# Sums of weight quarters by accumulating DMAs instead of GpSimd, in a two-layer trunk on one core

## The chip, the cores and the metric

The kernel runs on one core of a Trainium2 chip. The core has a matrix engine (TensorE, PE in the profile), three engines for elementwise work (VectorE or DVE, ScalarE or ACT, GpSimd or POOL), and a queue engine (SyncE, SP) that issues most transfers. All transfers are carried by 16 DMA engines that the queues share. The metric is device time in microseconds; the kernel before takes 1237.47 us in the median of three runs (1236.72 to 1238.4).

## The reference

The input x has 512 tokens of 1024 features. There are two layers, each with a mixer, an MLP and a gate; every one of them sits between RMS norms and is added to x. All is float32.

```python
for i in range(2):
    m = fox_attention(hn, ...) if i == 0 else short_conv(hn, ...)     # hn = rmsnorm(x, g[0])
    x = x + rmsnorm(m, g[1])
    f = jnp.square(jax.nn.relu(rmsnorm(x, g[2]) @ w_mlp_up[i])) @ w_mlp_down[i]
    x = x + rmsnorm(f, g[3])
    gate = jax.nn.sigmoid(rmsnorm(x, g[4]) @ w_ple_gate[i])
    x = x + rmsnorm((p[i] @ w_ple_proj[i]) * gate, g[5])
```

The up weight is 1024 x 4096, the down weight 4096 x 1024. The change concerns the down weight, `wdn` in the kernel.

## The kernel before, in words

**Precision.** Each float32 matrix is split in two parts of a shorter type that the matrix engine multiplies faster: `split` (L272, L273) has ScalarE write the high part `wh` and another engine subtract it from the source to give the low part `wl`. `mm3` (L264 to L266) then issues three matmuls per product: high by high, low by high, high by low.

**The MLP.** The 4096 hidden features go in eight groups of 512 per layer, `up(gr)` and then `down(gr)`. In `up`, four tiles f = 0 to 3 of 128 features are computed over all 512 tokens with 24 matmuls each; ScalarE applies relu and square (L825, L811). For groups 0 to 6 `down` is a fast matrix product of the Strassen-Winograd kind: with the activations cut in quarters A11 to A22 and the group's down weight in quarters B11 to B22, seven products of half size replace eight. It needs four sums of activations, S1 to S4, which GpSimd forms in `quarters` (L839) as each f is done, and four sums of weights, T1 to T4. Each T is two tiles of 128 x 512 (p = 0, 1). The products run in the order of `STEPS`: 1 (B11), 2 (B21), 4 (T4), 5 (T1, with S1), 6 (T2), 7 (T3), 3 (B22), with 12 matmuls each. Their results are summed over the groups in `acc`, and after group 6 `combine` (L878) adds the seven sums up on GpSimd. Group 7 is an ordinary product.

**The weights' way.** Every weight tile is an item in one list in the order of use. `prepare` walks it a few items ahead of use (`SOON` = 8): `fetch` (L157) has SP load the 256 KB tile into one of 14 `raw` buffers, and `split` puts the halves into two of 70 `pages`, buffers of 2 KB per partition that almost everything shares. When `prepare` reaches a group's first down item, `derive` has all eight quarter tiles loaded and has GpSimd form the T tiles, eight subtractions of 128 x 512 per group (L167); GpSimd also splits the T tiles (L273, eight per group). Fourteen groups use it, seven per layer.

**What orders the work.** Only parts of the attention's start and end are written in a fixed order. Elsewhere a scheduler, which works from estimates of the instructions' times, orders each engine's instructions at build time; an instruction whose buffer is free early can be placed far ahead of its use. On the chip each engine and each queue runs its list strictly in that order. SP has at most eight transfers under way: each waits for the eighth before it.

**The start.** The attention's first stage norms four blocks of 128 tokens, t = 0 to 3. For each, ScalarE sums squares (L295), GpSimd forms the reciprocal root `n_r` in two small instructions (L287, L290), VectorE scales the block to `n_h` (L303), TensorE transposes it (`n_p`, L312), and ScalarE and VectorE split it into `hTh` and `hTl`. The orders of TensorE, VectorE and ScalarE are written out there; GpSimd's and SP's are not. VectorE's list has `n_h` of t = 3 ahead of `hTl` of t = 2. TensorE computes the values `v` of block t in between.

Of the kernel before, what the change touches and what calls it, by code (L numbers as in the profile page):

```python
# [8 lines left out]
F32 = mybir.dt.float32  # L9
F32R = mybir.dt.float32r  # L10
AF = mybir.ActivationFunctionType
ALU = mybir.AluOpType
# [3 lines left out]
P = 128  # L16
D = 1024
S = 512
# [7 lines left out]
PUT_OFF = 46000  # L26
LAG = 2
AHEAD = 2
PAGES = 70
RAWS = 14  # L30
LEAD = 1
V_CHUNKS = ((768, 272), (0, 512), (512, 256))
# [13 lines left out]
PRODUCTS = {  # L46
    1: ("A11", "B11"), 2: ("A12", "B21"), 3: ("S4", "B22"), 4: ("A22", "T4"),
    5: ("S1", "T1"), 6: ("S2", "T2"), 7: ("S3", "T3"),
}
STEPS = (1, 2, 4, 5, 6, 7, 3)  # L50
# [18 lines left out]
def trunk(ctx: ExitStack, tc, x, pT, g, wv, wqk, bf, wo, wci, wcq, cw, wco, wup, wdn, wpp, wpg, out):  # L69
    nc = tc.nc  # L70
    pool = lambda name, bufs, **k: ctx.enter_context(tc.tile_pool(name=name, bufs=bufs, **k))
    consts = pool("consts", 1)
    raws = pool("raws", RAWS)
    normed = pool("normed", 1)
    pages = pool("pages", PAGES)
    small = pool("small", 8)
    psum = pool("psum", 8, space=PSUM)
    dram = pool("dram", 1, space=DRAM)

    def page(name, dtype=F32):  # L80
        return pages.tile([P, S], dtype, tag="pg", name=name)
# [14 lines left out]
    loads, order, where, ready, fetched, begun = [], [], {}, {}, [], [0]  # L96
    derived, recipes = {}, {}
# [9 lines left out]
    def plan_sums(key, forms, quarters, sums):  # L107


        at = {}  # L110
        for name, src in quarters:
            at[name] = len(loads)
            loads.append(src)
        for name in forms:
            where[(*key, *name)] = len(order)
            order.append(((*key, *name), at.get(name, key)))
        recipes[key] = at, sums

    def plan_down(l, gr):

        plan_sums(
            ("dn", l, gr),
            [(PRODUCTS[i][1], p) for i in STEPS for p in range(2)],
            [
                ((name, p), wdn[l, c, 4 * gr + 2 * p + r])
                for name, r, c in (("B11", 0, 0), ("B21", 1, 0), ("B12", 0, 1), ("B22", 1, 1))
                for p in range(2)
            ],
            [
                ((name, p), (a, p), (b, p), ALU.subtract)  # L130
                for p in range(2)
                for name, a, b in (("T1", "B12", "B11"), ("T3", "B22", "B12"),
                                   ("T2", "B22", "T1"), ("T4", "B21", "T2"))
            ],
        )

    def plan_sevens(key, srcs):
        plan_sums(
# [18 lines left out]
            nc.sync.dma_start(raw[:, : src.shape[-1]], src)  # L157

    def derive(key):
        at, sums = recipes.pop(key)  # L160
        fetch(max(at.values()) + 1)
        B = {name: fetched[n][:, :S] for name, n in at.items()}
        for name, a, b, op in sums:
            t = page("_".join(str(u) for u in (*key, *name)))
            derived[(*key, *name)] = t
            B[name] = t[:, :S]
            ins = nc.gpsimd.tensor_tensor(out=B[name], in0=B[a], in1=B[b], op=op)  # L167
            if last_norm:
                tc.add_manual_dep(
                    ins.ins, last_norm.pop().ins.name,  # L170
                    mybir.DependencyInfo(mybir.DependencyClass.Sync, mybir.DependencyReason.DATA),
                )
# [30 lines left out]
    for l in range(2):  # L203
# [10 lines left out]
        else:  # L214
# [3 lines left out]
            for i in range(2, KT, 2):  # L218
                for name in "ucb":
                    s = "cub".index(name)  # L220
# [586 lines left out]
    def mlp(l, hT, xs, then, late):  # L807
        acc = {}
# [27 lines left out]
        def quarters(gr, f, q, s, A):  # L836

            L, R = slice(0, S // 2), slice(S // 2, S)
            sums = lambda out, a, b, op: nc.gpsimd.tensor_tensor(out=out, in0=a, in1=b, op=op)  # L839
            if f % 2 == 0:  # L840
                s[f] = page(f"s34{l}_{gr}_{f}")
                sums(s[f][:, L], q[f][:, L], q[f][:, R], ALU.subtract)
                return
            left, right = q[f - 1], q[f]
            halves(gr, f, ("A12", "A22"), right, A)
            s12, s34 = page(f"s12{l}_{gr}_{f}"), s[f - 1]
            sums(s12[:, L], left[:, R], right[:, R], ALU.add)
            sums(s12[:, R], s12[:, L], left[:, L], ALU.subtract)
            sums(s34[:, R], right[:, L], s12[:, R], ALU.subtract)
            halves(gr, f, ("S1", "S2"), s12, A)  # L850
            halves(gr, f, ("S3", "S4"), s34, A)
# [21 lines left out]
        def combine():  # L873

            for s in range(2):
                for to, i in ((2, 1), (6, 1), (7, 6), (4, 7), (6, 5), (3, 6), (5, 7)):
                    a = acc[to, s][:, :S]
                    nc.gpsimd.tensor_tensor(out=a, in0=a, in1=acc[i, s][:, :S], op=ALU.add)  # L878
            return {
                (2 * half + s, n): acc[i, s]  # L880
                for s in range(2) for i, half, n in ((2, 0, 0), (3, 0, 1), (4, 1, 0), (5, 1, 1))
            }

        for gr in range(7):
            A, s, q = {}, {}, {f: page(f"q{l}_{gr}_{f}") for f in range(4)}
# [9 lines left out]
            down(gr, A)  # L895

        total, hs, gB = combine(), [], []

        def done(f, lo, hi, r):
# [12 lines left out]
        for t in range(NB):  # L912
# [6 lines left out]
            for n in range(2):  # L919
                a = total[t, n][:, :S]  # L920
                nc.vector.tensor_tensor(out=a, in0=banks[n], in1=a, op=ALU.add)
            fs = [total[t, n][:, :S] for n in range(2)]
            sums = [squares(f, f"fs{l}_{t}_{n}") for n, f in enumerate(fs)]
# [183 lines left out]
```

## Time and profile before

| | |
|---|---|
| median of three runs | 1237.47 us (1236.72 to 1238.4) |
| profiled execution: its span (no other time is recorded for it) | 1235.8 us |
| TensorE matmul busy | 1213.4 us, 98% |
| VectorE, ScalarE, GpSimd busy | 896.5, 676.1 and 686.8 us |
| moved by DMA | 148.73 MB, 120 GB/s in the mean |
| granted TensorE clock | 0.998 |

The span is from the first to the last instruction; the runs' median lies 1.67 us above it. Busy time is a sum over instructions; the list of waits tells how long an engine stood before an instruction and what released it. In a timeline row the first number is the start in us, the second the duration of the row's instructions together, and xN their count; idle time ahead of them stands in brackets.

### The profile page before, as it was taken

To read this page: it belongs to the slowest core of one execution; us is meant where nothing else is said; L and a number is where in the kernel's file an instruction comes from. 1 tells how busy PE (TensorE), PEld (TensorE's weight loads), DVE (VectorE), ACT (ScalarE), POOL (GpSimd) and SP (SyncE) were. 2 spreads that over 40 slices of the span, in tenths; PEclk is the share of its full clock that TensorE was granted. 3 is DMA by queue.
4 is the path that set the end of the run, shared out by engine and by line. 5 is a ranking of instruction groups with operands and counts; after the bars stand their busy time and mean duration, and the time that the engine had idled before them with its cause. 6 is when DMAs were issued, how large, how long until landed. Compare 5 with 4: busy or idle time off the path is not lost.

```text
span 1235.8 us, 18684 instructions
## 1 busy us (share of the span) xinstructions
PE 1213.4 (98%) x6188; PEld 1030.6 (83%) x6188; DVE 896.5 (73%) x1394; ACT 676.1 (55%) x1429; POOL 686.8 (56%) x667
## 2 busy tenths in 40 slices
PE   7999999999999999999999999999999999999997
PEld 6888888888888888888889999989778888888885
DVE  5657878675667667869877798865767787669873
ACT  5457777556635654465566544445756345635551
POOL 2016667247878777775213255317778868778210
PEclk9999999999999999999999999999999999999999
DMA  7456564442343224428133033552412443235401
GB/s 253 150 160 169 147 159 114 151 164 66 115 137 98 88 88 136 123 69 288 67 102 107 27 107 96 154 176 71 136 59 78 137 136 95 66 114 178 163 18 52
DMA packets 85793, 148.73 MB, mean 120 GB/s; under 512 B 10112, under 2 KB 17328, under 8 KB 85696
## 3 DMA queue, kind: packets, MB, share of 16 engines
q1 hardware_dynamic: 85488, 147.27, 38.7%
q8 instruction: 49, 0.80, 0.3%
q14 instruction: 48, 0.39, 0.1%
q10 hardware_dynamic: 144, 0.26, 0.1%
q0 software_dynamic: 64, 0.00, 0.0%
HBM read 136.93 MB, written 6.37 MB: 116 GB/s over the span
## 4 chain that ended last, share of the span: by engine, by line
PE 89%; DVE 3%; POOL 2%; ACT 2%; issue 2%; DMA 2%; SPq 0%; POOLq 0%; DVEq 0%; ACTq 0%
PE up L266 9%; PE up L265 9%; PE up L264 9%; PE dn L265 8%; PE dn L266 8%; PE dn L264 8%; PE pg L265 2%; PE pg L264 2%; PE pg L266 2%; PE qk L264 2%; PE qk L265 2%; PE qk L266 2%; PE co L264 1%; PE co L266 1%; PE co L265 1%
## 5 line engine op out<-in xcount | busy, mean ns | idle before, releaser
L273 DVE TENSOR_TENSOR wl<-raw,wh 128x512 fp32r<-128x512 f32 (+1 forms) x398 | 370.2, 975 | 27.5 <-ACT wh L272 26.3
L272 ACT CAST wh<-raw 128x512 fp32r<-128x512 f32 (+1 forms) x398 | 217.1, 620 | 4.6 <-DVE xd L348 4.4
L265 PE MATMUL up<-hTh,wl 128*128 128x512 f32 (+1 forms) x576 | 210.2, 365 | 0.0
L266 PE MATMUL up<-hTl,wh 128*128 128x512 f32 (+1 forms) x576 | 209.7, 366 | 0.3 <-DVE hTl L273 0.3
L264 PE MATMUL up<-hTh,wh 128*128 128x512 f32 (+1 forms) x576 | 209.4, 366 | 0.0
L273 POOL TENSOR_TENSOR wl<-dn_T,wh 128x512 fp32r<-128x512 f32 x112 | 155.0, 1417 | 32.6 <-ACT wh L272 32.6
L825 ACT ACTIVATE r<-up 128x512 f32<-128x512 f32 (+1 forms) x72 | 39.4, 547 | 200.4 <-PE up L266 200.4
L871 DVE TENSOR_TENSOR acc<-dn,acc 128x512 f32<-128x512 f32 x168 | 107.2, 678 | 23.9 <-PE dn L266 23.9
L265 PEld LDWEIGHTS up<-hTh,wl 128*128 128x128 f32 x576 | 108.6, 189 | 17.7
L264 PEld LDWEIGHTS up<-hTh,wh 128*128 128x128 f32 x576 | 108.6, 189 | 17.5
L266 PEld LDWEIGHTS up<-hTl,wh 128*128 128x128 f32 x576 | 108.3, 189 | 17.9 <-DVE hTl L273 0.5
L167 POOL TENSOR_TENSOR dn_T<-raw,raw 128x512 f32<-128x512 f32 x56 | 87.5, 1575 | 58.9 <-DMA raw<-in_wdn 39.6
L167 POOL TENSOR_TENSOR dn_T<-raw,dn_T 128x512 f32<-128x512 f32 x56 | 93.3, 1666 | 2.2
L272 ACT CAST wh<-dn_T 128x512 fp32r<-128x512 f32 x112 | 61.4, 616 | 11.0 <-POOL dn_T L167 11.0
L273 DVE TENSOR_TENSOR A12l<-q,A12h 128x512 fp32r<-128x512 f32 x28 | 23.3, 833 | 51.7 <-ACT A12h L272 51.7
L273 DVE TENSOR_TENSOR A11l<-q,A11h 128x256 fp32r<-128x256 f32 x28 | 25.9, 926 | 45.5 <-ACT A11h L272 45.5
L878 POOL TENSOR_TENSOR acc<-acc,acc 128x512 f32<-128x512 f32 x28 | 46.9, 1706 | 9.9 <-DVE acc L871 9.9
L264 PE MATMUL qk<-hTh,wh 128*128 128x512 f32 x128 | 51.1, 399 | 0.0
L266 PE MATMUL qk<-hTl,wh 128*128 128x512 f32 x128 | 50.8, 397 | 0.0
L265 PE MATMUL pg<-wh,hTl 128*128 128x512 f32 x128 | 50.5, 394 | 0.0
L264 PE MATMUL pg<-wh,hTh 128*128 128x512 f32 x128 | 50.4, 394 | 0.0
L265 PE MATMUL qk<-hTh,wl 128*128 128x512 f32 x128 | 50.2, 393 | 0.0
(372 smaller groups left out, 3240.3 us busy)
## 6 DMA issues: line engine op xcount, KB each, us to landing
raw<-in_wup SPq DMA_DIRECT2D x128, 256.0 KB, 3.0
raw<-in_wdn SPq DMA_DIRECT2D x128, 256.0 KB, 2.9
raw<-in_wcq SPq DMA_DIRECT2D x36, 256.0 KB, 2.9
raw<-in_wqk SPq DMA_DIRECT2D x32, 256.0 KB, 3.6
raw<-in_wpg SPq DMA_DIRECT2D x32, 256.0 KB, 4.0
g<-in_g SPq DMA_DIRECT2D x22, 256.0 KB, 5.8
prl<-neg_c SPq DMA_DIRECT2D x16, 256.0 KB, 7.0
raw<-in_wo SPq DMA_DIRECT2D x16, 256.0 KB, 4.0
```

The lines of the kernel that those rows point to most:

```text
L167: ins = nc.gpsimd.tensor_tensor(out=B[name], in0=B[a], in1=B[b], op=op)
L264: nc.tensor.matmul(ps, a.hi, b.hi, start=start, stop=False)
L265: nc.tensor.matmul(ps, a.lo, b.hi, start=False, stop=False)
L266: nc.tensor.matmul(ps, a.hi, b.lo, start=False, stop=stop)
L272: nc.scalar.copy(hi, src)
L273: eng.tensor_tensor(out=lo, in0=src, in1=hi.bitcast(F32), op=ALU.subtract)
L825: nc.scalar.activation(r[:, :n], ps[:, :n], AF.Relu)
L871: nc.vector.tensor_tensor(out=a, in0=banks[s], in1=a, op=ALU.add)
L878: nc.gpsimd.tensor_tensor(out=a, in0=a, in1=acc[i, s][:, :S], op=ALU.add)
```

## The change

The sums T1 to T4 are no longer formed by GpSimd instructions. For each T, both tiles together, SP loads one quarter (512 KB, two rows of 2 KB per partition) into a buffer of a new pool `sums` of five buffers, and a DMA issued from GpSimd's queue adds the second term to it in place: from HBM for T1 and T3, from the buffer of T1 for T2 and of T2 for T4. [...] B12 is no longer loaded as tiles of its own, since only the T need it. GpSimd still splits the T tiles. The wait that held the first sum behind the last norm is gone from this part. `PAGES` falls from 70 to 60, which pays for the five buffers.

```diff
-PAGES = 70
+PAGES = 60
+SUMS = 5
...
+    def add_up(l, gr):
+
+        block = lambda r, c: wdn[l, c, 4 * gr + r : 4 * gr + r + 3 : 2].rearrange("k p c -> p k c")
+        B11, B21, B12, B22 = (block(r, c) for c in range(2) for r in range(2))
+        T = {}
+        for name, first, second in (("T1", B11, B12), ("T3", B12, B22),
+                                    ("T2", B22, "T1"), ("T4", B21, "T2")):
+            T[name] = t = sums.tile([P, 2, S], F32, tag="sum", name=f"{name}_{l}_{gr}")
+            nc.sync.dma_start(t, first)
+            second = T[second] if isinstance(second, str) else second
+            nc.gpsimd.dma_start(t, second, accum_op=ALU.add)
+        for name, t in T.items():
+            for p in range(2):
+                derived["dn", l, gr, name, p] = t[:, p, :]
...
     def derive(key):
+        if key[0] == "dn":
+            add_up(*recipes.pop(key))
+            return
         at, sums = recipes.pop(key)
...
-                sums(s[f][:, L], q[f][:, L], q[f][:, R], ALU.subtract)
+                sums(s[f][:, L], q[f][:, R], q[f][:, L], ALU.subtract)
...
-            sums(s12[:, L], left[:, R], right[:, R], ALU.add)
-            sums(s12[:, R], s12[:, L], left[:, L], ALU.subtract)
+            sums(s12[:, L], right[:, R], left[:, R], ALU.subtract)
+            sums(s12[:, R], s12[:, L], left[:, L], ALU.add)
...
-                for to, i in ((2, 1), (6, 1), (7, 6), (4, 7), (6, 5), (3, 6), (5, 7)):
-                    a = acc[to, s][:, :S]
-                    nc.gpsimd.tensor_tensor(out=a, in0=a, in1=acc[i, s][:, :S], op=ALU.add)
+                for to, i, j, op in (
+                    (2, 2, 1, ALU.add), (6, 6, 1, ALU.subtract), (7, 7, 6, ALU.add),
+                    (4, 4, 7, ALU.subtract), (6, 6, 5, ALU.subtract), (3, 3, 6, ALU.add),
+                    (5, 7, 5, ALU.subtract),
+                ):
+                    a, b, c = (acc[k, s][:, :S] for k in (to, i, j))
+                    nc.gpsimd.tensor_tensor(out=a, in0=b, in1=c, op=op)
```

More of the change, by code (lines that the diff above doesn't have):

```diff
@@ L119, in plan_down @@
     def plan_down(l, gr):
[L121 to L135, printed above, removed]
+        key = "dn", l, gr
+        at = {}
+        for name, r, c in (("B11", 0, 0), ("B21", 1, 0), ("B22", 1, 1)):
+            for p in range(2):
+                at[name, p] = len(loads)
+                loads.append(wdn[l, c, 4 * gr + 2 * p + r])
+        for i in STEPS:
+            for p in range(2):
+                name = PRODUCTS[i][1]
+                where[(*key, name, p)] = len(order)
+                order.append(((*key, name, p), at.get((name, p), key)))
+        recipes[key] = l, gr
+    def add_up(l, gr):
[9 more added lines that the diff above has]
+        for name, t in T.items():
+            for p in range(2):
+                derived["dn", l, gr, name, p] = t[:, p, :]
     def plan_sevens(key, srcs):
```

1 line of the change is left out of this document (added).

## The prediction

> **What bounds the kernel now.** I read the page's busy times first, then the list of TensorE's waits, then busy time by stage.
>
> ```profile
> PE 1213.4 (98%) x6188; PEld 1030.6 (83%) x6188; DVE 896.5 (73%) x1394; ACT 676.1 (55%) x1429; POOL 686.8 (56%) x667
> ```
> ```profile
> PE dn L264 <- ACT r L825: 1.1, 2, 0.9
> ...
> PE dn L265 <- DVE S1l L273: 0.8, 2, 0.4
> ...
> PE dn L265 <- DVE A12l L273: 0.4, 1, 0.4
> PE up L266 <- DVE hTl L273: 0.3, 1, 0.3
> ```
> ```profile
> core 0: us, PE busy (x) PEld busy (x) DVE busy (x) ACT busy (x) POOL busy (x), PEclk, DMA share, GB/s
> 275.00:300.00 25.00, 24.01 (x157) 21.36 (x157) 14.23 (x14) 14.84 (x34) 21.82 (x20) 1.00 0.22 65
> 300.00:382.00 82.00, 81.51 (x358) 66.58 (x357) 51.34 (x61) 50.39 (x95) 65.64 (x50) 1.00 0.33 103
> 382.00:590.00 208.00, 208.00 (x920) 172.22 (x919) 160.73 (x198) 107.27 (x198) 151.09 (x115) 1.00 0.43 136
> 850.00:870.00 20.00, 19.62 (x122) 17.10 (x121) 9.24 (x10) 10.57 (x24) 17.19 (x16) 1.00 0.23 66
> 870.00:952.00 82.00, 81.24 (x356) 66.34 (x356) 57.78 (x60) 51.72 (x98) 64.72 (x51) 1.00 0.34 103
> ```
>
> TensorE is the bound: 1213.4 of 1235.8 us. In the MLP's later groups (382 to 590) it has no idle time at all, and a matmul takes 208/920 = 0.226 us. What idles in the two MLPs is 0.99 + 0.49 us in the first groups of layer 0 and 0.38 + 0.76 us in those of layer 1, 2.62 us together. Whatever the change frees on GpSimd can give back 2.62 us at most; the rest of its work lies beside a full TensorE. A delay at the kernel's start, ahead of all this, is added to the end whole.
>
> **GpSimd's relief: 0 to -2.62 us, taken as -1.0.**
>
> ```profile
> L167 POOL TENSOR_TENSOR dn_T<-raw,raw 128x512 f32<-128x512 f32 x56 | 87.5, 1575 | 58.9 <-DMA raw<-in_wdn 39.6
> L167 POOL TENSOR_TENSOR dn_T<-raw,dn_T 128x512 f32<-128x512 f32 x56 | 93.3, 1666 | 2.2
> ```
>
> 112 subtractions go, 87.5 + 93.3 = 180.8 us of GpSimd, 12.9 us per group. The splits of the T stay. In a first group the eight sums stand at the head of a chain (sums, casts, splits, activation sums) that ends in the waits on r, S1l and A12l above. In the changed program the sums of layer 0's first group are placed in the attention's first 40 us and those of layer 1's at the end of layer 0's MLP, so this head is gone. The waits named add up to 2.3 us, but they are on ScalarE's and VectorE's work, whose queues also change order here. I take 1.0 of the 2.62, about the wait on r.
>
> **The start: this is the term that decides.** The five `sums` buffers are free from the beginning, so the scheduler has placed five of the new loads and five accumulating DMAs at the kernel's start. Two places in the built order matter. SP has the load of T1 at the place where the small load `taps` stood (taps moves behind). GpSimd has the accumulation of T1 between the `n_r` of block 2 and that of block 3, and GpSimd must stand there until the T1 load has landed. Behind it wait `n_r` of block 3, then `n_h` of block 3, and behind that, in VectorE's written order, `hTl` of block 2, which TensorE needs next.
>
> ```profile
> 16.71 0.33 SPq L685 DMA_DIRECT2D taps<-in_cw  x1
> 17.44 1.01 SPq L157 DMA_DIRECT2D raw<-in_wv  x2
> 18.78 25.31 SPq L157 DMA_DIRECT2D raw<-in_wqk  x18
> ```
> ```profile
> raw<-in_wdn SPq DMA_DIRECT2D x128, 256.0 KB, 2.9
> ...
> taps<-in_cw SPq DMA_DIRECT2D x1, 12.0 KB, 5.0
> ```
> ```profile
> 15.00:20.00 5.00, 3.99 (x25) 3.21 (x25) 3.78 (x6) 3.77 (x10) 1.73 (x4) 1.00 1.05 391
> ```
> ```profile
> 20.33 0.30 POOL L287 TENSOR_SCALAR n_r_v<-n_q,n_q 128x1 f32<-128x1 f32 x1 [2.74 <-ACT junk L295]
> 20.71 0.56 POOL L290 TENSOR_TENSOR n_r_y<-n_r_v,neg_half 128x1 f32<-128x1 f32 x1
> 21.23 0.53 POOL L643 MEMSET ones<- 128x512 f32 x1
> ```
> ```profile
> 21.31 1.41 DVE L303 SCALAR_TENSOR_TENSOR n_h<-xc,n_r_y,g 128x512 f32<-128x512 f32 x2 [1.08 <-POOL n_r_y L290]
> 22.82 1.29 DVE L273 TENSOR_TENSOR hTl<-n_p,hTh 128x512 fp32r<-128x512 f32 x2
> ...
> 37.15 0.42 DVE L648 CAST tri<-ones 128x512 fp32r<-128x512 f32 x1
> ```
> ```profile
> 23.56 0.29 PE L264 MATMUL v<-wh,hTh 128*128 128x272 f32 x1
> 23.69 0.29 PE L265 MATMUL v<-wh,hTl 128*128 128x272 f32 x1
> ```
>
> T1's load is issued at 16.71, where taps was. The DMA engines are full there (share 1.05, 391 GB/s): taps, 12 KB, took 5.0 us to land, because what was issued before it came first. T1 stands behind the same transfers and is 524 KB itself, 1.34 us at 391 GB/s: it lands at 16.71 + 5.0 + 1.34 = 23.05. Then GpSimd issues the accumulation, which holds it for D; then come the two `n_r` instructions, which before began at 20.33. Everything behind is late by 23.05 + D - 20.33 = 2.72 + D. The first half of `hTl` ends at 22.82 + 0.65 = 23.47 and TensorE reads it at 23.69, a slack of 0.22. TensorE's stall is therefore 2.50 + D.
>
> ```profile
> L972 POOL DMA_DIRECT2D row<-in_g x2: 497/623/749, 1.4 to 2.1; - x2
> ```
> ```profile
> q0 software_dynamic: 64, 0.00, 0.0%
> ```
>
> D has no row: the trace has no accumulating DMA. The nearest are GpSimd's two small DMAs, 0.50 and 0.75 us each, with 64/2 = 32 packets. That is the lower end, 0.5. If all of the 0.62 grew with the packets, the 256 rows of 2 KB of a sum would take 0.62 x 256/32 = 5.0, the upper end. SP's issues take 0.33 us for 12 KB as for a full tile (1.01 for two and the wait between them), so most of an issue is fixed; I take 1.2, an estimate near the lower end. The stall is then 3.7 us (3.0 to 7.5).
>
> The Trainium skill (DMA: Bandwidth & Descriptors, section "Anatomy of one DMA — SWDGE (gpsimd) path") puts a transfer at about 2.0 us plus its bytes at 436 GB/s, 3.2 us for 512 KB. By that T1 would land at 19.9, before `n_r` of block 3 is due, the stall would be 0.5 us and the sum -0.5 instead of +2.7. The trace does not agree for this place: taps' 12 KB took 5.0 us.
>
> **What else moves.**
> - `ones`, from which `tri` is made at 37.15, now stands behind the accumulation of T2, which waits for T1's to finish. SP issues the last of the five loads when T1 has landed, 23.05, as the last of eight transfers then outstanding (four of 0.52 and four of 0.26 MB, 3.1 MB): 8.0 us at 391 GB/s, and 2.7 us more for the 1.05 MB that T1's and T3's accumulations move, so 33.8. Two more issues of D and `ones` with its mask (0.53 us, and as much again) end at 37.3. `tri` is due at 37.15 + 3.7 = 40.9. Covered by 3.6 us; without that, VectorE and the weight splits behind `tri` lose the excess.
> - The `wqk` loads stand behind the sums' 2.6 MB, 6.7 us at 391 GB/s. They are first used past 50 us.
> - In each later group GpSimd loses 12.9 us of sums and gets four issues, 4.8 us at 1.2. SP loses two loads of 256 KB and gets four of 512 KB; with the accumulations a group moves 3.7 MB more. Over its 180 x 0.226 = 40.7 us that is 90 GB/s on 136, below the 391 that the engines showed. Hidden.
> - 70 to 60 pages: in both built orders the shortest stretch from the release of a page to the first matmul that reads the weight half written there is 59 matmuls, 13 us. Nothing.
> - The signs cost nothing: the same instructions with other operands.
> - The MLP's later GpSimd order has the accumulation of the next T3 between the activation sums of f = 2 and f = 3:
>
> ```profile
> 413.77 0.74 POOL L839 TENSOR_TENSOR s<-q 128x256 f32<-128x256 f32 x1
> 415.18 0.74 POOL L839 TENSOR_TENSOR s<-q,q 128x256 f32<-128x256 f32 x1 [0.66 <-ACT q L811]
> ```
>
> GpSimd waits for ScalarE's q there, so f = 3 has just ended, at about 414.4, and product 5 is 36 matmuls, 8.1 us, away: 422.5. From 415.18 the two sums (0.74 each), cast and split (about 0.7 each) are done at 418.1. The slack is 4.4 us. T3's load waits for the split of the T4 before, whose pages came free at the end of the last `down`, some 20 us earlier, so that only D counts, and 1.2 is hidden.
>
> Sum: +3.7 - 1.0 = +2.7 us against the profiled execution, 1235.8 to 1238.5. Carrying the 1.67 us between span and median, 1237.47 + 2.7 = **1240.2 us**.
>
> **The rivals.**
> - *The T1 load is not late.* If it lands as the unhurried 256 KB loads do (2.9 us, and 0.67 for the other half), at 20.28, the stall is 20.28 + 1.2 - 20.33 - 0.22 = 0.9, the sum -0.1: 1237.4. Against it: share 1.05 and the 5.0 us. Chance 0.20.
> - *Faster.* The first groups give back all 2.62 and the start costs nothing: 1234.8. It needs T1 landed by 20.33 + 0.22 - D = 19.35 us; from there on each further us is lost. For it: the sums do head that chain. Chance 0.06.
> - *The clock falls.*
> ```profile
> 11.85 0.59 PE L264 MATMUL v<-wh,hTh 128*128 128x272 f32 x1
> ...
> 15.46 0.43 PE L265 MATMUL v<-wh,hTl 128*128 128x272 f32 x1
> 15.68 0.43 PE L266 MATMUL v<-wl,hTh 128*128 128x272 f32 x1
> ```
>   At the kernel's start, after idling, matmuls of 272 columns came 0.22 us apart (15.46, 15.68) for the 3.8 us from 11.85 on; at 23.56 they come 0.13 apart. If the 3.7 us stall brings that pace back for as long, about 1.7 us more are lost: 1241.9. Against it: the granted clock reads 1.00 in the row from 15 to 20 with the slow pace in it, so the row can't tell, and no later gap of this length exists to show it. The Trainium skill (TensorE: Matmul & The Clock Gate, "Part 1: The HAM clock gate (the "warmup" mystery)") has the clock fall to half after a whole idle window of some 3.4 us; by that a stall of 3.7 us is just long enough, if it meets the window's phase. Chance 0.12.
> - *An issue costs more than 4.4 us.* Then each of 13 groups stalls at product 5. With D = 5.0 that is 13 x 0.6 = 7.8, and the start costs 7.5: 1237.5 + 7.5 + 7.8 - 1.0 = 1251.8. Below 4.4 it costs nothing there. Chance 0.10.
>
> **How the numbers follow.** The forecast has 0.52, the rivals 0.20, 0.06, 0.12 and 0.10. A change of 0.2%, 2.5 us, is about what a measurement of this kernel tells from none. The forecast's own range is 1237.9 (stall 3.0, all 2.62 back) to 1242.5 (D = 2.5, nothing given back). About two thirds of it are slower by over 2.5 us: 0.35, with the last two rivals 0.57. Faster keeps 0.06, and 0.37 is left. The range runs from 1237.0, which takes in most of the hidden load, to 1246, which takes in the clock and dear issues up to about half the way to that rival.
>
> **What would show it.** Right: an idle stretch of TensorE of about 3.7 us near 24 us, released by VectorE's `hTl`, which `n_h` and `n_r` held up; an accumulating issue of about 1.2 us just ahead of `n_r` of block 3; the first groups' idle of 2.62 us down to about 1.6; GpSimd's busy time down by about 180 us less the issues; later groups still without idle time. Wrong: T1 landing before 20.3, waits of `dn` on S1l in the later groups, or pages or weight tiles among TensorE's waits.

## The result: 1.8% slower, and not where the change does its work

The changed kernel takes 1259.81 us in the median (1258.28 to 1259.97, four runs) against 1237.57 us before on the same chip (1236.72 to 1238.4): a ratio of 1.0176, with a 95% interval of 1.0164 to 1.0188. The forecast was 1240.2, the upper end of its range 1246.0. The span of the profiled execution is 1258.0 us, 22.2 more than before.

First the page's busy times of the changed kernel.

```profile
PE 1223.7 (97%) x6188; PEld 1037.9 (83%) x6188; DVE 830.9 (66%) x1394; ACT 677.4 (54%) x1429; POOL 562.4 (45%) x611
```

GpSimd is relieved as reckoned: 686.8 - 562.4 = 124.4 us fewer. Its new issues cost 28 x 1.218 + 28 x 0.903 = 59.4 us, so the 180.8 us of subtractions are gone, to within 3 us. TensorE has the same 6188 matmuls. The busy time by stage (columns as in the prediction: busy us and count of PE, PEld, DVE, ACT, POOL, then granted clock, share of the DMA engines, GB/s) shows where it stands still.

```profile
0.00:25.00 25.00, 16.42 (x77) 12.65 (x77) 9.77 (x19) 13.66 (x33) 6.91 (x18) 0.93 0.90 314
25.00:60.00 35.00, 32.85 (x171) 28.47 (x172) 23.69 (x63) 16.11 (x43) 5.44 (x8) 0.95 0.92 252
...
255.00:300.00 45.00, 45.00 (x306) 41.58 (x305) 26.33 (x40) 27.04 (x63) 20.99 (x28) 1.00 0.48 135
300.00:382.00 82.00, 82.00 (x364) 67.89 (x363) 42.26 (x60) 49.79 (x94) 43.73 (x42) 1.00 0.68 191
382.00:590.00 208.00, 208.00 (x919) 172.05 (x918) 141.79 (x192) 105.24 (x194) 116.64 (x100) 1.00 0.74 211
...
640.00:680.00 40.00, 35.19 (x191) 29.73 (x190) 26.91 (x40) 23.89 (x60) 8.29 (x17) 0.91 0.16 47
...
850.00:870.00 20.00, 14.52 (x95) 14.11 (x96) 13.70 (x23) 8.87 (x22) 3.42 (x6) 0.84 0.36 112
870.00:952.00 82.00, 82.00 (x416) 70.28 (x416) 43.23 (x61) 50.68 (x100) 43.22 (x41) 1.00 0.67 187
```

The MLPs' first groups (255 to 382, 870 to 952) are full now and the later ones stayed full. These rows show losses in three stretches: at the start, at 640 to 680 (the gate of layer 0) and at 850 to 870 (layer 1's first `up`). Only the first was foreseen.

Where the time went shows best when the same matmul is looked for in both traces: the start of the k-th TensorE matmul of a kernel, less the start of the k-th of the kernel before. Both have 6188, and their order differs only by some places here and there, so a delay is good to about 1 us. The columns are times in the kernel before, `end` is the last matmul; the kernels below the first row are the experiments that follow.

| delay in us at | 35 | 268 | 348 | 606 | 680 | 802 | 845 | 916 | end |
|---|---|---|---|---|---|---|---|---|---|
| changed kernel | 5.0 | 3.5 | 0.5 | 1.2 | 11.6 | 14.6 | 23.9 | 22.0 | 22.8 |
| e1_pages60 | 0.0 | -0.3 | 0.0 | 0.6 | 10.8 | 13.9 | 21.9 | 22.2 | 23.1 |
| e5_pages64 | 0.0 | -0.9 | -0.9 | -0.4 | 9.3 | 9.8 | 16.6 | 17.0 | 18.4 |
| e4_pages66 | 0.7 | -0.6 | -0.4 | 0.0 | 9.3 | 9.2 | 15.8 | 16.5 | 17.8 |
| e10_pages68 | -0.4 | -0.7 | -0.4 | -0.5 | 2.5 | 2.5 | 6.3 | 7.5 | 7.6 |
| e2_sums_in_pages | 0.0 | -0.5 | 15.2 | 45.0 | 48.3 | 48.3 | 48.3 | 62.3 | 95.2 |
| e3_no_early_sums | 0.0 | -0.4 | 18.3 | 18.8 | 29.1 | 32.1 | 40.2 | 38.1 | 38.9 |
| e3_ahead1 | 3.4 | 2.4 | -0.6 | 0.3 | 11.0 | 14.5 | 22.3 | 20.2 | 21.0 |
| e6_ahead1_late_sum | 0.0 | -1.2 | -4.2 | -3.4 | 7.2 | 10.8 | 18.6 | 17.1 | 17.9 |
| e7_pair_weights_in_sums | 6.2 | 4.2 | 1.3 | 1.3 | 0.5 | 4.5 | 11.8 | 10.3 | 10.2 |
| e8_pair_weights_late_sum | 0.0 | -1.5 | -4.4 | -4.4 | -5.3 | -1.3 | 6.3 | 5.2 | 5.2 |
| e9_both_in_sums_late_sum | 0.0 | -1.2 | -4.1 | -4.1 | -4.1 | 2.9 | 8.0 | 5.4 | 5.4 |
| e11_no_ahead_at_co | 0.0 | -1.7 | -4.6 | -4.6 | -5.5 | -1.5 | 5.6 | 3.6 | 3.6 |
| e12_gains_in_sums | 0.0 | -0.6 | -3.5 | -3.5 | 0.1 | 2.9 | 6.1 | 4.1 | 4.1 |
| e13_all_late_sums | 0.9 | 0.2 | -2.8 | -2.8 | -3.7 | -0.9 | 2.9 | 1.2 | 1.2 |

In the changed kernel the delay is 1.2 us at 606 us and grows by 22.7 us up to 845 us: 10.4 at the gate, 3.0 in layer 1's mixer (680 to 802 us) and 9.3 at its output and just behind. 1.1 us are won back behind that. No sum of weight quarters is used between 606 and 845 us.

**The start**, GpSimd's and VectorE's rows and TensorE's waits of the first 40 us (total, times, longest):

```profile
22.71 1.31 POOL L146 DMA_DIRECT2D T<-in_wdn  x1 [5.12 <-DMA T<-in_wdn]
24.11 0.29 POOL L304 TENSOR_SCALAR n_r_v<-n_q,n_q 128x1 f32<-128x1 f32 x1
24.49 0.57 POOL L307 TENSOR_TENSOR n_r_y<-n_r_v,neg_half 128x1 f32<-128x1 f32 x1
```
```profile
25.09 1.41 DVE L320 SCALAR_TENSOR_TENSOR n_h<-xc,n_r_y,g 128x512 f32<-128x512 f32 x2 [4.86 <-POOL n_r_y L307]
26.41 1.28 DVE L290 TENSOR_TENSOR hTl<-n_p,hTh 128x512 fp32r<-128x512 f32 x2
```
```profile
PE v L282 <- DVE hTl L290: 2.4, 1, 2.4
PE n_p L329 <- DVE n_h L320: 1.8, 1, 1.8
```

GpSimd stands 5.12 us for the T1 load, then issues for 1.31 us; `n_r` of block 3 comes after it, and `n_h` and `hTl` follow in VectorE's order. This is the predicted chain, row for row.

Of TensorE's two waits only the one of 2.4 us belongs to it. The other ends at 16.92 us, before the accumulation, and the kernel before has it at the same place. First TensorE's rows of the changed kernel, then the row of the kernel before, then the changed kernel's busy time in two stretches (columns as above).

```profile
16.92 1.77 PE L329 MATMUL n_p<-ident,n_h 128*128 128x128 f32 x8 [1.81 <-DVE n_h L320]
...
27.15 0.39 PE L282 MATMUL v<-wh,hTl 128*128 128x272 f32 x1 [2.42 <-DVE hTl L290]
```
```profile
16.92 1.31 PE L312 MATMUL n_p<-ident,n_h 128*128 128x128 f32 x8 [0.81 <-DVE n_h L303]
```
```profile
17.10:20.50 3.40, 3.40 (x17) 3.26 (x17) 3.03 (x5) 2.32 (x5) 0.48 (x1) 0.51 1.05 393
...
27.30:30.70 3.40, 3.40 (x16) 3.40 (x17) 2.74 (x7) 0.53 (x2) 0.00 (x0) 0.52 1.10 265
```

So the delay of 5.0 us at 35 us has three parts. 0.9 us come before the stall: in the changed kernel the granted clock is 0.51 from 17.1 to 20.5 us, behind the wait for `n_h`. e4_pages66, which has none of the new DMAs, and e13, which has them late, lose 0.7 and 0.9 us there, so this part is not the sums'. The matmul that the prediction named, at 23.69 before, starts at 27.15, 3.46 us late, so the stall adds some 2.6 us. The other 1.5 us are the clock again, 0.52 from 27.3 to 30.7 us.

**The gate of layer 0.** ScalarE's rows of the changed kernel, then of the kernel before. The names: `wh<-raw` is the high part of a weight prepared ahead, `gate` the activation of a gate block.

```profile
629.81 0.60 ACT L289 CAST wh<-raw 128x512 fp32r<-128x512 f32 x1
638.54 1.98 ACT L289 CAST wh<-raw 128x512 fp32r<-128x512 f32 x3 [8.12 <-PE pg L282]
640.58 0.60 ACT L977 ACTIVATE gate<-pg 128x512 f32<-128x512 f32 x1
```
```profile
627.00 2.17 ACT L272 CAST wh<-raw 128x512 fp32r<-128x512 f32 x4
629.08 0.59 ACT L956 ACTIVATE gate<-pg 128x512 f32<-128x512 f32 x1
```

Three of four casts wait 8.12 us for a page, and the activations stand behind them in ScalarE's list, so the third gate block's activation comes 11.5 us later than before (640.58 against 629.08; the kernel was 1.2 us late already). On it hang, one behind the other, the product with the gate, the residual, the next norm's `n0b_h` and its transposition, for which TensorE then waits.

**Layer 1's mixer output**, ScalarE and VectorE of the changed kernel, then the first of four such casts in the kernel before, which come one by one and wait for nothing:

```profile
834.54 2.67 ACT L289 CAST wh<-raw 128x512 fp32r<-128x512 f32 x4 [6.81 <-PE co L283]
```
```profile
835.20 2.73 DVE L290 TENSOR_TENSOR wl<-raw,wh 128x512 fp32r<-128x512 f32 x4 [7.56 <-PE co L283]
```
```profile
825.85 0.61 ACT L272 CAST wh<-raw 128x512 fp32r<-128x512 f32 x1
```

It is the same picture: four casts and four subtractions wait for pages, the residual and the norm stand behind. TensorE's waits between 600 and 900 us show the ends of these chains first (total, times, longest); the kernel before has no wait above 0.7 us there:

```profile
PE n_p L329 <- DVE n_h L320: 3.9, 1, 3.9
PE n0b_p L329 <- DVE n0b_h L320: 3.0, 1, 3.0
PE up L283 <- DVE hTl L290: 1.6, 1, 1.6
```

**The granted clock** falls behind waits of TensorE (0.93 and 0.95 in the two rows of the start, 0.91 and 0.84 at the two late places, 1.00 elsewhere in the rows above). TensorE's timeline at the gate:

```profile
655.49 2.29 PE L329 MATMUL n0b_p<-ident,n0b_h 128*128 128x128 f32 x8 [2.95 <-DVE n0b_h L320]
...
658.95 0.63 PE L282 MATMUL pg<-wh,hTl 128*128 128x512 f32 x1
659.38 0.63 PE L283 MATMUL pg<-wl,hTh 128*128 128x512 f32 x1
659.81 0.63 PE L281 MATMUL pg<-wh,hTh 128*128 128x512 f32 x1
```

Matmuls of 512 columns come 0.43 us apart here, where an undisturbed one takes 0.226. By these rows about (1 - 0.91) x 40 = 3.6 us are lost this way at the gate and (1 - 0.84) x 20 = 3.2 us at the head of layer 1's MLP, beside waits of 3.0 and of 3.9 + 1.6 us.

### The profile page after: what moved, and what is told of

Same layout as the page of the kernel before. It is cut to its first block, busy times and chain, and to the rows that moved or that the text cites. A ratio compares the mean times of both kernels' runs of the same rounds, so it can differ in the third digit from the quotient of the medians.

```text
span 1258.0 us, 18811 instructions
## 1 busy us (share of the span) xinstructions
PE 1223.7 (97%) x6188; PEld 1037.9 (83%) x6188; DVE 830.9 (66%) x1394; ACT 677.4 (54%) x1429; POOL 562.4 (45%) x611
## 4 chain that ended last, share of the span: by engine, by line
PE 89%; DVE 4%; ACT 2%; issue 2%; DMA 1%; POOL 1%; SPq 0%; DVEq 0%; POOLq 0%; ACTq 0%
PE up L283 9%; PE up L281 9%; PE up L282 9%; PE dn L281 8%; PE dn L282 8%; PE dn L283 8%; PE qk L282 2%; PE qk L281 2%; PE qk L283 2%; PE pg L282 2%; PE pg L283 2%; PE pg L281 2%; PE n_p L329 1%; PE pT L557 1%; PE o L283 1%
## 5 line engine op out<-in xcount | busy, mean ns | idle before, releaser
L290 DVE TENSOR_TENSOR wl<-raw,wh 128x512 fp32r<-128x512 f32 (+1 forms) x398 | 302.3, 798 | 47.3 <-ACT wh L289 29.6
L290 POOL TENSOR_TENSOR wl<-T,wh 128x512 fp32r<-128x512 f32 x112 | 155.3, 1419 | 45.5 <-ACT wh L289 34.2
L282 PEld LDWEIGHTS up<-hTh,wl 128*128 128x128 f32 x576 | 109.7, 190 | 17.4
L290 DVE TENSOR_TENSOR A12l<-q,A12h 128x512 fp32r<-128x512 f32 x28 | 22.7, 810 | 108.4 <-ACT A12h L289 98.1
L290 DVE TENSOR_TENSOR A11l<-q,A11h 128x256 fp32r<-128x256 f32 x28 | 22.0, 786 | 62.0 <-ACT A11h L289 62.0
L856 POOL TENSOR_TENSOR s<-q 128x256 f32<-128x256 f32 x28 | 20.6, 734 | 93.2 <-ACT q L828 93.2
L289 ACT CAST wh<-T 128x512 fp32r<-128x512 f32 x112 | 61.2, 616 | 0.0
L290 DVE TENSOR_TENSOR S1l<-s,S1h 128x512 fp32r<-128x512 f32 x28 | 28.0, 1002 | 48.8 <-ACT S1h L289 48.8
L146 POOL DMA_DIRECT2D T<-in_wdn x28 | 34.1, 1218 | 55.9 <-DMA T<-in_wdn 28.6
L856 POOL TENSOR_TENSOR s<-q,q 128x256 f32<-128x256 f32 x28 | 26.6, 951 | 56.0 <-ACT q L828 56.0
```

The costliest lines, as they stand in the source:

```text
L146: nc.gpsimd.dma_start(t, second, accum_op=ALU.add)
L282: nc.tensor.matmul(ps, a.lo, b.hi, start=False, stop=False)
L289: nc.scalar.copy(hi, src)
L290: eng.tensor_tensor(out=lo, in0=src, in1=hi.bitcast(F32), op=ALU.subtract)
```

## The experiments

Theory A, in its first form: the ten pages that the sums pool took are the cause, through a wait for a page that stands in a strict queue ahead of what TensorE needs. The rivals: the sums by DMA cost the time (B in the first two expectations); fewer pages cost in proportion (B from e3_ahead1 on); or the order that was planned for TensorE is to blame (C).

### Pages alone: e1_pages60

```diff
-PAGES = 70          # in the kernel before
+PAGES = 60
```

> The kernel before with 60 pages instead of 70 and nothing else changed: GpSimd still forms the sums. Theory A (the pages): in the changed kernel's trace ScalarE stands 8.1 us at 630 us before a weight cast that has no free page, with the gate's activations behind it in its queue, and between 632 and 877 us the changed kernel falls 23 us behind. If the pages alone do that, this kernel is slower by 18 to 24 us (1.015 to 1.019 of before), with the same idle time ahead of a cast in the gate of layer 0. Theory B (the new loads and accumulations rearrange the schedule or crowd the DMA engines there): this kernel is within 4 us of before.

Measured: 1260.43 us against 1237.02, ratio 1.0185 (1.017 to 1.020). The kernel before with ten pages fewer loses what the changed kernel loses. ScalarE shows the same wait at the same place:

```profile
637.90 1.99 ACT L272 CAST wh<-raw 128x512 fp32r<-128x512 f32 x3 [8.13 <-PE pg L265]
```

Its delay is within 1 us of zero up to 606 us and then runs as the changed kernel's. So the sums by DMA, with all they bring, come out at about -1 us (1.0176 against 1.0185, intervals overlapping), and the first rival is out.

### The sums without the sums pool: e2_sums_in_pages

```diff
-PAGES = 60
-SUMS = 5
+PAGES = 70
...
-            T[name] = t = sums.tile([P, 2, S], F32, tag="sum", name=f"{name}_{l}_{gr}")
-            nc.sync.dma_start(t, first)
+            for p in range(2):
+                T[name, p] = t = page(f"{name}_{l}_{gr}_{p}")
+                nc.sync.dma_start(t[:, :S], block(*first, p))
```

Each T is two pages with a load and an accumulating DMA of 256 KB each.

> The changed kernel with the pool of sums given back: 70 pages, each T tile is a page again, filled by a 256 KB load and a 256 KB accumulating DMA (16 such pairs a group's half as large instead of 4 of 512 KB in two steps each; eight pairs a group). The built order has no sum ahead of the MLP, so the start is as before. Theory A (the pages): the loss between 632 and 877 us is gone, and what is left is the first groups' idle time of 2.6 us given back, less what the sums cost at the head of the MLP: 1234 to 1238 us, ratio 0.997 to 1.001. Theory B (loads and accumulations, which are as many bytes here): 1250 to 1262 us.

Measured: 1335.27 us, ratio 1.0784 (1.0764 to 1.0804); neither theory had that. Its 45 us up to 606 us come group by group in the MLP. From 606 to 845 us it loses 3.3 us, where the changed kernel loses 22.7, which agrees with A, but the run is spoilt as a test: without a pool of its own a T is loaded only when its group begins, and GpSimd's list has the accumulations ahead of the activation sums:

```profile
323.59 0.88 POOL L145 DMA_DIRECT2D T<-in_wdn  x1 [11.26 <-DMA T<-in_wdn]
...
332.25 1.06 POOL L852 TENSOR_TENSOR s<-q 128x256 f32<-128x256 f32 x1
```

GpSimd stood 11.26 us for a load, with the first activation sum of the next f behind it.

### The sums not at the start: e3_no_early_sums

```diff
+                if l == 0 and gr < 2:      # each T load after the last norm of the attention's output
+                    tc.add_manual_dep(ins.ins, norm[0].ins.name, ...)
```

> The changed kernel (60 pages, five sum buffers) with the loads of layer 0's first two groups made to wait for the last norm ahead of the MLP, so that none stands in the attention's start. It takes the start's stall away (in the changed kernel TensorE is 5.0 us behind at 35 us, and 1.6 us at 308 us). If the start's stall is worth what it measures there, 1254 to 1255; if the attention takes most of it up again, as the gap of 1.6 us at 308 says, 1256 to 1258, or no gain at all where the sums now stand at the head of the MLP. On the pages it tells nothing: the loss after 630 us stays in either theory.

Measured: 1277.65 us, ratio 1.0329 (1.0312 to 1.0346), so this was missed. The stall of the start is gone (0.0 at 35 us), but the sums now come too late for the first group:

```profile
ACT wh L296 <- DMA T<-T: 23.4, 1, 23.4
PE dn L288 <- ACT A11h L296: 14.7, 1, 14.7
```

A cast on ScalarE waits 23.4 us for a sum, and the activations that TensorE needs stand behind it. The delay at 348 us is 18.3. From 606 us on it runs as the changed kernel's. The early place of the sums is worth much more than the stall that it brings.

### Less prepared ahead: e3_ahead1, and how many pages: e4_pages66, e5_pages64

```diff
-FEW = 4             # the changed kernel; weights prepared ahead in the second half of the columns
+FEW = 1
```
```diff
-PAGES = 70          # the kernel before
+PAGES = 66          # e4; 64 in e5
```

> The changed kernel with 60 pages, but in the second half of the columns of a mixer output and of a gate only 1 weight is prepared ahead instead of 4 (FEW = 1). Theory A (a cast that waits for a page stands in ScalarE's queue ahead of the gate's activation, and in VectorE's ahead of the residual; the pages themselves are not short): nothing waits in those queues, the 23 us between 632 and 877 us come back but for what TensorE then waits for late weights; the delay against the kernel before, +1.5 us at 632 us, stays about that to the end: 1237 to 1243 us. Theory B (60 pages are too few for the work in flight, in proportion): less is prepared ahead, TensorE waits for weights, and the time stays at 1258 to 1265 us.

> The kernel before with 66 pages in place of 70. At 60 pages one of the four casts at the gate of layer 0 still found a page and three waited, so it was short by 6 pages; at layer 1's mixer output all four waited, so it was short by 8. Theory A: at 66 the gate of layer 0 is clear of the wait and one weight still waits at the mixer output of layer 1, which is enough to hold the queue: of the 23 us the part up to 719 us (13) is gone and the part from there to 877 us (10) stays: 1244 to 1249 us. Theory B, in proportion to the pages missing (4 of 10): 1246 us, with the loss spread over both places.

> The kernel before with 64 pages. Theory A: one weight of four waits at the gate of layer 0, and the wait of one holds the queue as long as that of three, so nearly the whole loss is there: 1255 to 1261 us, with a ScalarE wait of about 8 us for a page at the gate. Theory B, in proportion (6 of 10): 1251 us.

Measured: e3_ahead1 took 1259.94 us, ratio 1.017 (1.0154 to 1.0185); 66 pages 1255.74 (1.0137, 1.0122 to 1.0153); 64 pages 1255.65 (1.0137, 1.0122 to 1.0152). Only the run with 64 pages came out where A had put it. e3_ahead1 contradicts A as it stood: no cast waited at the gate any more, and the time was the same, where B had put it; with 66 pages it was 7 us more than A allowed. B in turn had 1251 and 1246 us for 64 and 66 pages, too low by 5 and 10. The rows tell why: something else waits for the same event. With 64 pages it is still a cast, with 66 (as in e3_ahead1) the gate's own activation:

```profile
637.50 0.62 ACT L272 CAST wh<-raw 128x512 fp32r<-128x512 f32 x1 [7.08 <-PE pg L265]
```
```profile
637.97 0.60 ACT L956 ACTIVATE gate<-pg 128x512 f32<-128x512 f32 x1 [6.56 <-PE pg L265]
```

The matmuls of the first four gate blocks, this one among them, had all been issued by 630.5 us in the second of these, so the gate does not wait for its input; it waits for the page that it writes. What ends the wait is a matmul of the sixth block, the last to read the second half of the gate's weights (told apart by counting matmuls along the built order): it begins at 637.32 there, its second matmul is the last to read its first weight's high part and ends at 637.93, and the gate begins at 637.97. In the changed kernel these times are 637.88, 638.50 and, for the cast, 638.54. So it is the number of pages held at once that matters, whoever asks for the next. Counted in the code, the gate stage holds 32 pages of gate weights, 12 of the six weights of the small projection (`p`, `pp`), 8 of the residual and 4 of gains: 56, before any product, norm or weight ahead. The mixer output of layer 1 holds 32 of weights, 16 of the convolution's results, 8 and 4: 60.

### The start apart: e6_ahead1_late_sum

```diff
             ins = nc.gpsimd.dma_start(t, second, accum_op=ALU.add)
+            if start_r:     # the first one: after n_r of block 3
+                tc.add_manual_dep(ins.ins, start_r.pop().ins.name, ...)
```

> The kernel of e3_ahead1, and the first accumulating DMA goes behind the scale of the last block of the first norm in GpSimd's queue, by an added dependence of that DMA on it. If the predicted stall of the start is what it looked like, TensorE's wait of 2.4 us for hTl and 1.8 us for n_h near 27 us go, the delay of 3.6 to 5 us at 35 us goes, and what of it reaches the MLP (1.6 us at 308 us) goes too; with the first groups' idle of 2.6 us given back the time is 1234 to 1238 us, 1 to 3 us under e3_ahead1. If instead the delay at the start is swallowed by attention anyway, the time is that of e3_ahead1 within 0.7 us.

Measured: 1255.4 us, ratio 1.0142 (1.0124 to 1.016), 4.5 us under e3_ahead1 in the median. The 1234 to 1238 us expected had counted on e3_ahead1's cure and were missed with it; the expected 1 to 3 us under e3_ahead1 were exceeded. The delay at 35 us is 0.0 and at 348 us -4.2. (The wait of 1.8 us near 27 us that the expectation names was the one that ends at 16.92.) So the start costs what it seemed to, and without it the sums by DMA are a gain of some 4 us up to the end of the first MLP.

### Pages given back at one place: e7, with the start mended: e8

```diff
+            if key[0] == "p" or key[0] == "pp" and key[2:] != (1, 1):
+                both = sums.tile([P, 2, S], F32R, tag="sum", name=f"w{n}")
+                hi, lo = both[:, 0, :], both[:, 1, :]
+            else:
                 hi, lo = page(f"wh{n}", F32R), page(f"wl{n}", F32R)
```

The sums pool holds nothing at the gate, so five weights of that stage go there. e7 is the changed kernel with this edit alone; e8 has the edit of e6 beside it (and `FEW` at 4).

> The changed kernel, with five of the six weights of the small projection of the gate phase (names p and pp, two pages each) put into the five buffers of the sums pool, which hold nothing there; so the gate phase has the 10 pages again that the change took, and every other place has 60. In the runs with 60, 64 and 66 pages the first thing that found no page (casts of weights, or the gate's own output page) was served at the same event, 1.1 us after the last block that reads the second half of the gate's weights began. Theory A (the gate phase holds about 70 pages at once, and whatever asks for one too many stops a strict queue until that block): the 13 us between 632 and 719 us go, the 10 us at layer 1's mixer output and MLP start stay: 1244 to 1249 us. Theory C (the loss there has another cause, as the order that was planned for TensorE): 1257 to 1262 us.

> The kernel of e7_pair_weights_in_sums, and the first accumulating DMA behind the scale of the last block of the first norm, as in e6_ahead1_late_sum. That step alone moved the delay at 606 us from +0.5 to -3.5 us there. By theory A 4 us under e7_pair_weights_in_sums: 1240 to 1245 us. By theory C 1253 to 1258 us.

Measured: e7 1246.87 us, ratio 1.0077 (1.0064 to 1.009); e8 1242.5 us, 1.0045 (1.0033 to 1.0057). Both lie where A put them. From 606 to 680 us e7 loses -0.8 us where the changed kernel lost 10.4, with the same pool of 60 pages. So the pages missing at the gate are the cause there. How they cost the time is not quite parted from C: with 60, 64 and 66 pages TensorE's built order has the gate's first `n0b_p` 17 or 18 matmuls later than with 70 or 68, and in e7 it is back in its place. No run has the waits with the order of 70 pages, or that order's change without the waits. In the changed kernel TensorE reaches the next `n0b_p` 2.95 us before its input all the same, and that input hangs on the late activation.

### The step: e10_pages68

> The kernel before with 68 pages. 64 and 66 lost the same 17 us. Theory A: the loss is a step, with its edge where the last of the gate phase's demands just fits. If 68 fits at the gate: its 9 us are gone and the time is 1238 to 1247 us; if it does not, the same event serves the one that waits and the time is that of 64 and 66, 1255 us. Theory B, in proportion: 1242 us with part of the loss at each place.

Measured: 1244.56 us, ratio 1.0061 (1.0048 to 1.0074). That lies in A's range, which held B's 1242 too. At 68 pages no wait for a page shows at the gate, where the loss from 606 to 680 us is down to 3.0 us; 5.0 are lost from 802 to 916 us, where VectorE's product waits 6.0 us for its page. The losses at 60, 64, 66 and 68 pages are 23.4, 17.3, 17.4 and 7.4 us (medians, each against the kernel before of the same call): 64 and 66 cost the same, and two pages more save ten microseconds. That is a step, not theory B's slope, and it is seen in the row of four losses rather than in this run alone.

### Layer 1's mixer output: e9, e11, e12

```diff
+            if ... or key[0] == "co" and key[1] == 1 and key[2] < 5:    # e9: five more weights in sums
...
-  wide(kind, n, k, soon=soon(t, n))
+  wide(kind, n, k, soon=0 if kind == "co" and n else soon(t, n))       # e11: no weight ahead here
...
+  if l == 1 and i in (1, 2):                                           # e12: its two gains in sums too
+      both = sums.tile([P, 2, S], F32, tag="sum", name=f"g{l}_{i}")
```

All stand on e8; e12 holds e11's edit.

> The kernel of e8_pair_weights_late_sum, and at layer 1's mixer output five of the eight weights of the second half of its columns in the sums buffers as well. Theory A: the 10 us between 816 and 877 us go too: 1232 to 1237 us, under the kernel before. Against it stands that layer 1's first sums can only begin when those weights are read (near 830 us), four loads and four accumulations one behind the other of some 11 us each, so T4 is ready near 875 us, where the third product of the first group wants it: if that binds, TensorE waits at the head of layer 1's MLP as it did in e3_no_early_sums, and the time is 1240 to 1250 us.

> The kernel of e8_pair_weights_late_sum, and in the second half of the columns of layer 1's mixer output no weight is prepared ahead (0 instead of 4). In e8 four casts stood there in ScalarE's queue for 6.8 us and four subtractions in VectorE's for 7.5 us, until the last block that reads those columns' weights began. Theory A: without them the wait goes, unless the next thing asked for finds no page either (60 pages are the residual's 8, the gains' 4, the convolution's 16 and the weights' 32 alone). If it goes: 1233 to 1237 us; if the products' or the norm's pages wait at the same event: 1240 to 1243 us. Theory C (the loss there is not of pages): 1240 to 1243 us, with no wait of ScalarE or VectorE on the mixer output's matmuls near 812 to 819 us.

> The kernel of e11_no_ahead_at_co, and the two gains of layer 1's mixer output (two pages each) in two of the five sums buffers, which frees 4 pages there and holds back only the fourth sum of layer 1's first group. Theory A: with 8 pages not asked for and 4 freed the demand is below that of the kernel before, so what was left of the wait is gone: 1232 to 1236 us, below the kernel before. Theory C: 1240 to 1243 us.

Measured: e9 1240.42 us, ratio 1.003 (1.0019 to 1.0042); e11 1241.46 (1.0032, 1.002 to 1.0043); e12 1241.31 (1.0031, 1.0019 to 1.0043). None reached what A gave for a full cure, and e11 and e12 lie where C had put them, so the times alone do not speak for A here; the waits do. In e9 the wait of ScalarE's casts on the mixer output's matmuls was gone (one of 3.2 us for another page was left), and 2.5 us were lost from 802 to 916 us against 6.5 in e8. But the casts of the moved weights were now placed early in ScalarE's list and waited for their loads, ahead of the convolution's work, which lost 7.0 us from 680 to 802 us against 4.0:

```profile
ACT w L298 <- DMA raw<-in_wco: 13.3, 5, 6.9
```

In e11 no cast waits, and the products' page waits in their place, as it had been allowed for:

```profile
DVE com L367 <- PE co L292: 6.9, 1, 6.9
```

In e12 that is gone too: from 802 to 916 us the loss is 1.2 us against 6.5 in e8. But at the gate 3.6 us were lost, which e8 did not lose. GpSimd's rows:

```profile
661.89 1.27 POOL L146 DMA_DIRECT2D T<-in_wdn  x1 [4.02 <-DMA T<-in_wdn]
663.25 0.29 POOL L317 TENSOR_SCALAR n0b_r_v<-n0b_q,n0b_q 128x1 f32<-128x1 f32 x1
663.60 1.25 POOL L146 DMA_DIRECT2D T<-in_wdn  x1
664.38 1.08 POOL L320 TENSOR_TENSOR n0b_r_y<-n0b_r_v,neg_half 128x1 f32<-128x1 f32 x1
```

It is the start's stall once more: an accumulating DMA of layer 1's first group waits 4.02 us for its load, ahead of a norm's scale.

### Both waits gone: e13_all_late_sums

```diff
         ple(l, h4, xs, g5, then)
+        start_r[:] = last_r     # layer 1's first group after the last scale of this norm
```

The dependence now holds for all four accumulations of such a group.

> The kernel of e12_gains_in_sums, and the accumulating DMAs of layer 1's first group behind the last scale of layer 0's last norm in GpSimd's queue, as layer 0's first group stands behind the last scale of the first norm. In e12 the delay against the kernel before went from -3.5 us at 348 us to +0.4 at 672, while e8 without the waiting accumulations had -5.3 there. If that wait is the cause, the delay is -4 to -5 us at 672 us, and with e12's course behind it (+2.5 us to 802 us, +3.2 to 845 us, -2 in the MLP) the time is 1235 to 1238 us: no longer slower than the kernel before. If something else in that stage took the 4 us: 1240 to 1242 us.

Measured: 1236.72 us (1235.81 to 1238.15, eleven runs) against 1237.08, ratio 0.9994 (0.9985 to 1.0003): no longer slower, and not shown to be faster. The delay is -3.7 us at 680 us. So the 22 us are gone with 60 pages still in the pool, by edits that each aim at one wait. Not every loss is gone: 2.8 us are still lost in the convolution and 3.8 from there to 845 us, where TensorE waits 2.8 us for `n_h`, and the gains of the sums make up for them. The kernels with 60 pages all lose 2.8 us or more in the convolution, those with 64 or more at most 0.5; this was not followed further.

## Why the prediction was wrong

- **"70 to 60 pages: ... 59 matmuls, 13 us. Nothing."** This is the step that failed, and it is the whole loss. It measured the lead from the release of a page to the matmul that reads the weight written there. That lead is indeed long: between 600 and 900 us no weight comes more than 0.6 us late to TensorE. What counted is the time that a cast or an activation stands in ScalarE's or VectorE's strict list before it can write, and what stands behind it there. Pages alone cost 23 us (e1), and with pages given back at the gate its 10.4 us are gone (e7). The sign that the prediction named for this, pages among TensorE's waits, looked at the wrong engine.
- **"The start: this is the term that decides."** The mechanism and the size were right, but it did not decide. The accumulation began at 22.71 against 23.05 predicted for T1's landing; `n_r` of block 3 came at 24.11, 3.78 us late against 3.92; D was 1.31 there against 1.2. The matmul that reads `hTl` started 3.46 us late against 3.7; TensorE's wait was only 2.42, since the clock had made it 0.9 us late before. Of the 5.0 us of delay at 35 us the attention took up 1.5, which the prediction did not reckon with ("is added to the end whole"); 3.5 reached the MLP.
- **"GpSimd's relief: 0 to -2.62 us, taken as -1.0."** Too small. All idle time in the first groups went, and the delay fell by 3.0 us from 268 to 348 us and by 1.9 from 845 to 916, 4.9 us together, more than the upper end of 2.62. That end was read from TensorE's busy time alone; what made up the rest was not looked for.
- *"The clock falls."* The rival came true as a mechanism: behind the stall the granted clock was 0.52 for 3.4 us, which cost 1.5 us, against 1.7 reckoned. It came back at the two late places, where it cost about 3.6 + 3.2 us. Whether it follows a stall is luck by these traces: at the same place TensorE stood 3.07 us in e3_ahead1 with the clock at 1.00 behind it, and 3.36 us in e7 with 0.90 from 25 to 60 us, so that the delays at 35 us are 3.4 and 6.2 us.

```profile
26.93 0.39 PE L282 MATMUL v<-wh,hTl 128*128 128x272 f32 x1 [3.07 <-DVE hTl L290]
```
```profile
27.20 0.59 PE L286 MATMUL v<-wh,hTl 128*128 128x272 f32 x1 [3.36 <-DVE hTl L294]
```

By the rule of the Trainium skill that stood beside this rival (TensorE: Matmul & The Clock Gate, "Part 1: The HAM clock gate (the "warmup" mystery)"), the clock falls after a whole idle window of some 3.4 us. The trace does not agree: in the changed kernel it fell behind waits of 1.81 and 2.42 us.
- *"The T1 load is not late"* and *"Faster"* are out: TensorE's waits show the stall. By the rule of the Trainium skill that was set beside the stall (DMA: Bandwidth & Descriptors, "Anatomy of one DMA — SWDGE (gpsimd) path") T1 would have been there at 19.9; the accumulation that waited for it began 2.8 us later, so that the measurement decides against it for this crowded place. The rule is stated for GpSimd's transfers, and this load is SP's.
- *"An issue costs more than 4.4 us"* is out: 1.22 and 0.90 us. The list of lines and the DMA issues of the changed kernel (median us from issue to landing at the end of a row):

```profile
L146 POOL DMA_DIRECT2D T<-in_wdn x28 | 34.1, 1218 | 55.9 <-DMA T<-in_wdn 28.6 <-PE dn L283 18.9 <-DVE wl L290 5.4
L146 POOL DMA_DIRECT2D T<-T x28 | 25.3, 903 | 24.7 <-DMA T<-in_wdn 15.6 <-DMA T<-T 7.7 <-PE dn L283 1.3
```
```profile
raw<-in_wup SPq DMA_DIRECT2D x128, 256.0 KB, 6.8
...
T<-in_wdn POOLq DMA_DIRECT2D x28, 512.0 KB, 8.2
T<-T POOLq DMA_DIRECT2D x28, 512.0 KB, 6.7
```

- **Later groups, traffic, signs (the subtractions that the diff turns around), `ones`:** as predicted, hidden. 382 to 590 us is full (208.00) at 211 GB/s against 136; 90 more were reckoned, 75 came.

Without the page step the sum would have been some 4 us too high, an estimate: the changed kernel lies about 1 us under e1, where +2.7 had been predicted for the rest.

## What to carry to other kernels

When a change takes buffers from a shared pool, count what each stage holds at once and compare it with the pool; a lead measured at one consumer says nothing about the others. A wait for a free buffer is paid by everything behind it in that engine's list, so the last missing buffer costs nearly as much as the first three (10.2 us at the gate with 60 pages, 9.3 with 66), and the cure is to find a pool that is idle in that stage. A DMA issued from an engine that also does small work on the critical path waits for its input in that engine's list; put it behind that work by a dependence.

## What the runs showed of the hardware

VectorE's subtractions of the weight split, all shapes together, became faster when GpSimd stopped adding beside them: 975 ns before, 798 in the changed kernel.

```profile
L273 DVE TENSOR_TENSOR wl<-raw,wh 128x512 fp32r<-128x512 f32 (+1 forms) x398 | 370.2, 975 | 27.5 <-ACT wh L272 26.3
```
```profile
L290 DVE TENSOR_TENSOR wl<-raw,wh 128x512 fp32r<-128x512 f32 (+1 forms) x398 | 302.3, 798 | 47.3 <-ACT wh L289 29.6 <-PE pg L282 8.1 <-PE co L283 7.6
```

Every run whose GpSimd still forms the sums has 973 to 998 ns here (e1, e4, e5, e10), every run with the sums by DMA 764 to 798. The prediction gave this no place. The Trainium skill (SBUF — State Buffer, "Who interferes with whom") has a VectorE instruction with two SBUF inputs contend with a GpSimd instruction that reads SBUF; the trace agrees, with 18% of the mean.

The loads of the up weights landed 6.8 us after their issue, 3.0 before the change, beside accumulating transfers that take 8.2 and 6.7 us each; TensorE never waited for it in the MLP. And a stall of TensorE of 2.4 to 6 us, at a place that is full otherwise, cost 1.5 to 3.6 us more by the slower clock behind it in the changed kernel, but the stall of 3.07 us in e3_ahead1 cost nothing more.
